# Value products in parts for four attention units, exponential sums on GpSimd, and attention loads on the sync queue, in a hybrid encoder block

## The chip, the cores and the metric

The kernel runs on one core of a Trainium2 chip. The metric is the device time of one execution in microseconds (us); lower is better. One core has TensorE (matrix products), VectorE, ScalarE, GpSimd and a sync engine that only issues transfers. The profile calls them PE, DVE, ACT, POOL and SP; PEld is TensorE's weight load.

## The reference

One layer of an encoder over 2048 tokens and 16 learned meta tokens, 1024 wide, all in float32:

```
proj = rms_norm(h) @ w_in                      # q (4 heads), k, v (2 heads each), u (4 x 128)
q, k = axial_rope(rms_norm(q)), axial_rope(rms_norm(k))
attn = softmax(q k^T / sqrt(128)) v            # every token attends to all 2064 keys
four = real(fft2(u)) @ w_fourier               # per group of 128 channels
h = h + concat(rms_norm(attn), rms_norm(four)) @ w_out
h = h + relu(rms_norm(h) @ w_up)^2 @ w_down
out = rms_norm(h), without the meta tokens
```

The change touches the attention: scores, softmax and the product with the values.

## The kernel before, in words

*Precision.* Most products split both operands into a high part in a short float32 form (type R32) and a low part, the remainder. `Split` makes them: ScalarE copies src to hi, VectorE subtracts hi from src and writes lo. `mm3` (L81 to L83) then issues three matmuls: hi with hi, hi with lo, lo with hi. A few products use whole float32 operands in one matmul instruction of the program, which the profile shows as two records. The value product of the attention (L902) is one of these.

*Attention.* Keys stand on the partitions. A unit is 256 queries of two heads (512 columns) that share a key head; there are 16 units. Each unit has 17 steps: 16 tiles of 128 keys and one of 96 rows that holds the meta keys. `scores` computes a step's scores s from keys kt and queries q in three parts; ScalarE copies them to S, two tiles to a buffer of 128x1024 (11 such buffers), and VectorE keeps the running maximum M. After a unit's last step, TensorE transposes M, VectorE reduces it, and the maximum comes back as mb. `softmax` runs 20 steps behind the scores. On an even step VectorE subtracts mb from a pair's S (L893) and ScalarE takes the exponential in place (L894). On an odd step VectorE adds the pair to the running sum acc (L898 for the first, L900 for the others: seven adds for a unit), and TensorE multiplies the two tiles with the values vn into o (L902). At step 16, acc is folded into sum, which `finish` reduces over the keys to 1/l; it passes through memory (l_d) and comes back as rb, spread over all partitions; O times rb goes to memory as parts.

*What runs beside it.* The attention is a generator of steps. Other generators fill TensorE between its steps, and `mix` spreads so many attention steps evenly over a generator's own. First comes u_pass (projection of u), then fourier (the transform, with constant tables tab in a ring of six), out_f (the Fourier half of the output product: 16 rows of 128 tokens, two halves each), then out_a for three blocks of queries (the attention half). ULEAD, FLEAD and OLEAD are the attention steps that are to be issued by the end of the first three; each block of out_a then takes STEPS_A more. In out_f, each row needs parts yh and yl of the transform's output, its squares ysq, which GpSimd adds together (L1018), a small product pys on TensorE that sums them, and rs_f, a power on GpSimd (L194). VectorE's L1046 scales out_f's product pof by rs_f and adds it to x.

*Order.* Each engine takes its instructions in the order in which the program has them; the planner that records the program sets that order from the generators and may move an instruction past others of its engine. `tc.issue_after(x)` keeps an instruction behind x. Waits between engines go by semaphores. GpSimd issues the loads of keys (kt, L754), values (vn, L763; vm, L760), queries (q, L791) and tables (tab, L608) in its own queue; nearly all other transfers of this stretch are issued by the sync engine.

Of the kernel before, what the change touches and what calls it, by code (L numbers as in the profile page):

```python
# [19 lines left out]
P = 128  # L20
# [14 lines left out]
REM = 96  # L35
# [8 lines left out]
FLEAD = 102  # L44
OLEAD = 166
AHEAD_U = 8
STEPS_A = 38
T_BUFS = 6
F_BUFS = (6, 7)
WU_BUFS = 3  # L50
P_BUFS = 5
S_BUFS = 11
A_BUFS = 5
ORDER = "1265734"
# [31 lines left out]
def ins_of(x):  # L86
    return getattr(x, "ins", x)
# [49 lines left out]
def encoder_block(ctx: ExitStack, tc: tile.TileContext, x, meta, w_in, w_f,  # L137
# [49 lines left out]
    c_fo = lambda k: cols[:, 20 + k:21 + k]  # L187

    def rstd_of(pool, ss, n, width, tag, rows=P):

        ms = pool.tile([P, n], F32, name="ms_" + tag, tag="ms_" + tag, bufs=2 if pool is tp else 4)
        nc.vector.tensor_scalar(ms[:rows], ss, 1.0 / width, EPS, op0=ALU.mult, op1=ALU.add)
        rs = pool.tile([P, n], F32, name="rs_" + tag, tag="rs_" + tag, bufs=2 if pool is tp else 4)
        nc.gpsimd.tensor_tensor(rs[:rows], ms[:rows], mhalf[:rows, :n], op=ALU.pow)  # L194
        return rs
# [400 lines left out]
    def load_tables(tr):  # L596

        src, full, rest, n_tab = sources(tr)
        rem = ft.tile([P, NG, REM], F32, name=f"rem{tr}", tag="rem", bufs=1)
        nc.vector.memset(rem, 0.0)  # L600
        for o in (0, 32, 64):
            for lo, hi in rest:
                nc.vector.tensor_copy(rem[:, :, o:o + hi - lo], src[:, :, lo:hi])
                o += hi - lo
        tabs = []
        for nt in range(n_tab):
            t = ft.tile([P, 4, CHP], R32, name=f"tab{tr}_{nt}", tag="tab", bufs=T_BUFS)[:, :, :CH]
# [99 lines left out]
    def fourier():  # L707
        for par in range(2):
# [3 lines left out]
            for g in range(NG):  # L712
# [38 lines left out]
    def load_k(u, g, c):  # L751
        n = KC + (MR if c == 3 else 0)
        kt = ap.tile([P, 2, KCP if c == 3 else KC], R32, name=f"kt_{u}_{c}", tag=f"KT{c // 3}", bufs=1 if c == 3 else 3)
        nc.gpsimd.dma_start(kt[:, :, :n], k_d[:, g, :, c * KC:c * KC + n])  # L754
        return kt

    def load_v(u, g, c):
        if c == 4:
            vt = ap.tile([P, P], R32, name=f"vm_{u}", tag="VM", bufs=1)
            nc.gpsimd.dma_start(vt[:MR], v_m[:, g])  # L760
        else:
            vt = ap.tile([P, 4, P], F32, name=f"vn_{u}_{c}", tag="VT", bufs=4)
            nc.gpsimd.dma_start(vt, v_n[:, g, 4 * c:4 * c + 4])  # L763
        return vt
# [14 lines left out]

    held = {}  # L780

    def attention():
# [5 lines left out]
        def load_q(u):  # L788
            b, g = units[u]
            q = ap.tile([P, 2, 2, 256], R32, name=f"q_{u}", tag="q", bufs=2)  # L790
            nc.gpsimd.dma_start(q, q_d[b][:, :, 2 * g:2 * g + 2])  # L791
            return q.rearrange("p l h n -> p l (h n)")
# [73 lines left out]
        def softmax(u, i):  # L866
# [4 lines left out]
            if i == NT:  # L871
# [6 lines left out]
                nc.vector.tensor_tensor(hi[32:64], S[32:64], f32v(hi[32:64]), op=ALU.subtract)  # L878
                sm = s["sum"] = ap2.tile([P, 512], F32, name=f"sum_{u}", tag="pl", bufs=1)
                nc.vector.tensor_tensor(sm, acc[:, 0], acc[:, 1], op=ALU.add)  # L880
# [10 lines left out]
            if i % 2 == 0:  # L891
                mb = s["mb"].rearrange("p (o n) -> p o n", o=1).broadcast_to([P, 2, 512])
                nc.vector.tensor_tensor(S, S, mb, op=ALU.subtract)  # L893
                held["exp"] = ins_of(nc.scalar.activation(p, S, AF.Exp, scale=ISQ))  # L894
                return
            v = vt[j // 2]
            if j == 1:
                nc.vector.tensor_tensor(acc, s["S"][0], p, op=ALU.add)  # L898
            elif j > 0:
                held["sub"] = ins_of(nc.vector.tensor_tensor(acc, acc, p, op=ALU.add))  # L900
            for e in range(2):
                nc.tensor.matmul(s["O"], v[:, 2 * j % 4 + e], p[:, e], start=i + e == 1, stop=False)  # L902

        def finish(u):
# [93 lines left out]
    def out_f():  # L998
# [6 lines left out]
        def rows(t):  # L1005
# [11 lines left out]
            for n in (2, 1):  # L1017
                nc.gpsimd.tensor_tensor(sq[:, :n], sq[:, :n], sq[:, n:2 * n], op=ALU.add)  # L1018
            ops[t] = [hi, lo, sq]
# [822 lines left out]
```

## Time and profile before

| | us |
|---|---|
| median of 3 runs | 2239.28 (2238.01 to 2241.07) |
| profiled execution, its own time | 2236.94 |
| profiled execution, span from first to last instruction | 2235.2 |

The shares of the span that each engine is busy:

| engine | busy us | share | instructions |
|---|---|---|---|
| TensorE | 2219.0 | 99% | 9890 |
| weight load | 1752.8 | 78% | 9890 |
| VectorE | 1681.4 | 75% | 2260 |
| ScalarE | 1170.8 | 52% | 1991 |
| GpSimd | 255.8 | 11% | 301 |

An engine's row in the profile names a line of the kernel, an operation, and what it writes and reads (out<-in, without buffer numbers), with its shape; after the bar stand busy us, mean ns of one, and the idle time of the engine just before, with what ended it. Rows of the timeline begin with the start and the length in us. "x4" says that four instructions are merged in the row. TensorE's matmuls are pipelined: a record of 0.39 us does not keep the next one from starting after 0.23.

### The profile page before, as it was taken

The numbers are of one execution on the slowest core, as the hardware profiler recorded it, in microseconds if no ns is written. First come the engines' busy times: TensorE is split into PE (matmuls) and PEld (weight loads), VectorE is DVE, ScalarE is ACT, GpSimd is POOL, SyncE is SP. The second block draws the span as 40 slices with busy tenths as digits, with TensorE's granted clock in tenths as the row PEclk, the third lists the DMA queues.
The fourth block names the chain that finished last, engine by engine and source line by source line (L and its number), as shares of the span: only waits on it lengthen the run. The fifth ranks groups of instructions, "written<-read, shape, count | busy, mean of one in ns | idle before, by whom it ended". The sixth has DMA issues, their size and how long they took to land.

```text
span 2235.2 us, 27654 instructions
## 1 busy us (share of the span) xinstructions
PE 2219.0 (99%) x9890; PEld 1752.8 (78%) x9890; DVE 1681.4 (75%) x2260; ACT 1170.8 (52%) x1991; POOL 255.8 (11%) x301
## 2 busy tenths in 40 slices
PE   9999999999999999999999999999999999999998
PEld 7888867777777666677888888888888888888887
DVE  6566299999888989887676778679656555796795
ACT  6554255655554667677555654334455555443243
POOL 2223101012132212110000020000100000200000
PEclk9999999999999999999999999999999999999999
DMA  7685743345346434476767585434594434955442
GB/s 244 207 264 175 255 134 90 88 114 166 118 146 206 160 95 139 133 266 231 264 225 243 198 296 192 164 125 151 213 360 151 163 138 164 344 169 160 134 130 85
DMA packets 219914, 408.08 MB, mean 183 GB/s; under 512 B 19568, under 2 KB 97776, under 8 KB 218112
## 3 DMA queue, kind: packets, MB, share of 16 engines
q1 hardware_dynamic: 192000, 343.64, 45.9%
q0 software_dynamic: 27632, 62.41, 9.1%
q8 instruction: 78, 1.28, 0.2%
q14 instruction: 60, 0.49, 0.1%
q10 hardware_dynamic: 144, 0.26, 0.0%
HBM read 260.16 MB, written 146.08 MB: 182 GB/s over the span
## 4 chain that ended last, share of the span: by engine, by line
PE 45%; DVE 3%; DMA 3%; ACT 1%; issue 1%; SPq 0%; POOLq 0%; POOL 0%; DVEq 0%; ACTq 0%
PE dx L81 5%; PE dx L83 5%; PE dx L82 5%; PE dy L81 4%; PE dy L83 4%; PE dy L82 4%; PE ux L83 3%; PE ux L82 3%; PE ux L81 3%; PE uy L81 3%; PE uy L83 3%; PE uy L82 3%; DMA f_d<-lf 2%; DMA lf<-m_d 1%; DVE wul L72 1%
## 5 line engine op out<-in xcount | busy, mean ns | idle before, releaser
L71 ACT CAST ah<-a 128x1024 fp32r<-128x1024 f32 x108 | 113.0, 1050 | 263.7 <-PE dx L82 107.2
L902 PE MATMUL o<-S,vn 128*128 128x512 f32 x512 | 242.8, 595 | 0.0
L833 ACT COPY S<-s 128x512 f32<-128x512 f32 x256 | 147.8, 587 | 143.4 <-PE s L83 136.8
L83 PE MATMUL dx<-bh,al 128*128 128x512 f32 x496 | 192.5, 388 | 0.0
L82 PE MATMUL dx<-bl,ah 128*128 128x512 f32 x496 | 192.5, 388 | 0.0
L81 PE MATMUL dx<-bh,ah 128*128 128x512 f32 x496 | 192.5, 388 | 0.0
L83 PE MATMUL ux<-bf,wul 128*128 128x512 f32 x448 | 174.3, 389 | 0.7 <-DVE wul L72 0.7
L81 PE MATMUL ux<-bf,wuh 128*128 128x512 f32 x448 | 174.6, 390 | 0.0
L82 PE MATMUL ux<-bf,wuh 128*128 128x512 f32 x448 | 174.3, 389 | 0.0
L893 DVE TENSOR_TENSOR S<-S,mb 128x1024 f32<-128x1024 f32 x128 | 153.0, 1222 | 17.6 <-ACT mb L864 17.6
L894 ACT ACTIVATE S<-S 128x1024 f32<-128x1024 f32 x128 | 134.5, 1065 | 50.0 <-DVE S L893 48.8
L72 DVE TENSOR_TENSOR al<-a,ah 128x1024 fp32r<-128x1024 f32 x108 | 131.3, 1221 | 31.7 <-ACT ah L71 31.3
L81 PE MATMUL s<-q,kt 128*128 128x512 f32 (+1 forms) x272 | 151.0, 555 | 1.8 <-DMA kt<-k_d 1.0
L81 PE MATMUL dy<-bh,ah 128*128 128x512 f32 (+1 forms) x388 | 150.5, 388 | 0.0
L82 PE MATMUL dy<-bl,ah 128*128 128x512 f32 (+1 forms) x388 | 150.5, 388 | 0.0
L83 PE MATMUL dy<-bh,al 128*128 128x512 f32 (+1 forms) x388 | 150.5, 388 | 0.0
L902 PEld LDWEIGHTS o<-S,vn 128*128 128x128 f32 x512 | 93.3, 189 | 69.1 <-issue 58.5
L81 PE MATMUL uy<-bf,wuh 128*128 128x512 f32 x320 | 124.9, 390 | 1.2 <-ACT wuh L71 1.2
L82 PE MATMUL uy<-bf,wuh 128*128 128x512 f32 x320 | 124.8, 390 | 0.0
L83 PE MATMUL uy<-bf,wul 128*128 128x512 f32 x320 | 124.7, 390 | 0.0
L1306 ACT ACTIVATE c<-c 128x512 f32<-128x512 f32 x96 | 60.5, 631 | 121.4 <-DVE c L1354 117.8
L839 DVE TENSOR_TENSOR M<-M,S 128x1024 f32<-128x1024 f32 x96 | 117.8, 1227 | 7.3 <-ACT S L833 6.1
(330 smaller groups left out, 5576.5 us busy)
## 6 DMA issues: line engine op xcount, KB each, us to landing
a<-s_d SPq DMA_DIRECT2D x84, 512.0 KB, 3.8
R<-in_w_up_dram SPq DMA_DIRECT2D x32, 1024.0 KB, 5.5
s_d<-s SPq DMA_DIRECT2D x128, 256.0 KB, 2.1
s_d<-c SPq DMA_DIRECT2D x96, 256.0 KB, 2.7
d<-in_w_down_dram SPq DMA_DIRECT2D x48, 512.0 KB, 5.1
f_d<-lf SPq DMA_DIRECT2D x56, 256.0 KB, 3.1
bf<-f_d SPq DMA_DIRECT2D x7, 2048.0 KB, 13.8
hk<-ht_d SPq DMA_DIRECT2D x24, 512.0 KB, 4.8
```

What stands on the lines that cost most here:

```text
L71: self.high = nc.scalar.copy(hi, src)
L72: self.low = nc.vector.tensor_tensor(lo, src, f32v(hi), op=ALU.subtract)
L81: nc.tensor.matmul(out, a[0], b[0], start=first, stop=False, skip_group_check=chain)
L82: nc.tensor.matmul(out, a[0], b[1], start=False, stop=False, skip_group_check=chain)
L83: nc.tensor.matmul(out, a[1], b[0], start=False, stop=last, skip_group_check=chain)
L833: nc.scalar.copy(S[:, i % 2], ps)
L839: nc.vector.tensor_tensor(M, M, S, op=ALU.max)
L893: nc.vector.tensor_tensor(S, S, mb, op=ALU.subtract)
L894: held["exp"] = ins_of(nc.scalar.activation(p, S, AF.Exp, scale=ISQ))
L902: nc.tensor.matmul(s["O"], v[:, 2 * j % 4 + e], p[:, e], start=i + e == 1, stop=False)
L1306: nc.scalar.activation(dst, src, AF.Relu)
```

## The change

Three things are done, with numbers of the order set anew.

- In units 6 to 9 (PARTS) the value product takes parts. The values' four tiles of 128x512 are split once into vp (`value_parts`); of each pair, the two 128x512 halves of the exponentials are split into hi and lo (ph and pl, five buffers together), and mm3 takes the place of the whole matmul.
- The adds of pairs 1 to 6 into acc go to GpSimd. The last, of pair 7, stays on VectorE. `on_pool` keeps GpSimd's instructions from the attention's start on in the order of the program.
- kt, vn and q are loaded by the sync queue; vm and the tables stay on GpSimd. The tables of the third transform are asked for earlier.

sum is now written into acc, and rb uses the buffer of ph. OLEAD goes from 166 to 176 and STEPS_A from 38 to 35. The operation that O's product with rb is kept behind is now the subtraction in place of the sum.

```diff
-OLEAD = 166
+OLEAD = 176
-STEPS_A = 38
+STEPS_A = 35
+PARTS = (6, 7, 8, 9)
+VP_BUFS = 5
...
+    def on_pool(call, *args, **kw):
+
+        with tc.issue_after(held["pool"]) if "pool" in held else nullcontext():
+            held["pool"] = ins_of(call(*args, **kw))
...
-        nc.gpsimd.tensor_tensor(rs[:rows], ms[:rows], mhalf[:rows, :n], op=ALU.pow)
+        if pool is tp:
+            nc.gpsimd.tensor_tensor(rs[:rows], ms[:rows], mhalf[:rows, :n], op=ALU.pow)
+        else:
+            on_pool(nc.gpsimd.tensor_tensor, rs[:rows], ms[:rows], mhalf[:rows, :n], op=ALU.pow)
...
-            nc.gpsimd.dma_start(t, c_even[tr, nt] if tr < 2 else c_odd[tr - 2, nt])
+            on_pool(nc.gpsimd.dma_start, t, c_even[tr, nt] if tr < 2 else c_odd[tr - 2, nt])
...
             sn = transform(2 * par + 1)
+            if not par:
+                load_tables(2)
...
-        nc.gpsimd.dma_start(kt[:, :, :n], k_d[:, g, :, c * KC:c * KC + n])
+        nc.sync.dma_start(f32v(kt[:, :, :n]), k_d[:, g, :, c * KC:c * KC + n])
...
-            nc.gpsimd.dma_start(vt, v_n[:, g, 4 * c:4 * c + 4])
+            nc.sync.dma_start(vt, v_n[:, g, 4 * c:4 * c + 4])
...
-            nc.gpsimd.dma_start(q, q_d[b][:, :, 2 * g:2 * g + 2])
+            nc.sync.dma_start(f32v(q), q_d[b][:, :, 2 * g:2 * g + 2])
...
+        def value_parts():
+
+            for c in range(4):
+                t = op2.tile([P, 2, 512], R32, name=f"vp_{c}", tag=f"vp{c}")
+                split(t[:, 0], t[:, 1], KV["v", PARTS[0]][c].rearrange("p a d -> p (a d)"))
+                VP.append(t.rearrange("p l (a d) -> p l a d", d=P))
...
-                sm = s["sum"] = ap2.tile([P, 512], F32, name=f"sum_{u}", tag="pl", bufs=1)
+                sm = s["sum"] = acc[:, 0]
...
-            if j == 1:
-                nc.vector.tensor_tensor(acc, s["S"][0], p, op=ALU.add)
+            if j == NT // 2 - 1:
+                nc.vector.tensor_tensor(acc, acc, p, op=ALU.add)
             elif j > 0:
-                held["sub"] = ins_of(nc.vector.tensor_tensor(acc, acc, p, op=ALU.add))
+                on_pool(nc.gpsimd.tensor_tensor, acc, s["S"][0] if j == 1 else acc, p, op=ALU.add)
+            if u in PARTS:
+                if not VP:
+                    value_parts()
+                v = VP[j // 2]
+                for e in range(2):
+                    k = 2 * j % 4 + e
+                    hi, lo = (op2.tile([P, 512], R32, name=f"p{x}{e}_" + nm, tag="vh", bufs=VP_BUFS) for x in "hl")
+                    split(hi, lo, p[:, e])
+                    mm3(nc, s["O"], (v[:, 0, k], v[:, 1, k]), (hi, lo), i + e == 1, False)
+                return
...
-                rb = ap2.tile([P, 512], F32, name=f"rb_{u}", tag="rb", bufs=1)
+                rb = ap2.tile([P, 512], F32, name=f"rb_{u}", tag="ph", bufs=1)
```

How the change moves instructions is shown at three places in the middle of out_f. First TensorE, from one row's pys to the next score. Before (L1023 is pys, L902 the whole value product of a pair's two tiles):

```order
L83 MATMUL pof_1_5967<-wfp_1_5287,yl_5857 128x512
L1023 MATMUL pys_5980<-ones,ysq_5946 128x1 [waits DVE_49,Pool_49]
L902 MATMUL o_5718<-S_10_5472,vn_2_5176 128x512 x2
L81 MATMUL s_14_5998<-q_5427,kt_3_4783 128x512 [waits Activation_49]
L82 MATMUL s_14_5998<-q_5427,kt_3_4783 128x512
```

After (lines are shifted; L83 to L85 is mm3, ph and pl are the parts of the exponentials):

```order
L85 MATMUL pof_1_6836<-wfp_1_5307,yl_6666 128x512
L1053 MATMUL pys_6849<-ones,ysq_6796 128x1 [waits PE_49,Pool_49]
L83 MATMUL o_6770<-ph_9_3_6857,vp_5309 128x512 [waits Activation_49]
L84 MATMUL o_6770<-pl_9_3_6858,vp_5309 128x512 [waits DVE_49]
L85 MATMUL o_6770<-ph_9_3_6857,vp_5309 128x512
L83 MATMUL o_6770<-ph_9_3_6864,vp_5309 128x512 [waits Activation_49]
L84 MATMUL o_6770<-pl_9_3_6865,vp_5309 128x512 [waits DVE_49]
L85 MATMUL o_6770<-ph_9_3_6864,vp_5309 128x512
L83 MATMUL s_6_6873<-q_6416,kt_1_6399 128x512 [waits Activation_49]
```

Six matmuls stand where two whole ones stood, and they wait for ScalarE and VectorE at the place; pys waits for GpSimd in both. Second, GpSimd over two rows of out_f. Before (rs_f, the two adds of the squares, and a key load):

```order
L194 TENSOR_TENSOR rs_f<-ms_f,mhalf 128x1
L1018 TENSOR_TENSOR ysq_6223<-ysq_6223 128x256
L1018 TENSOR_TENSOR ysq_6223<-ysq_6223 128x128
L754 DMA kt_0_6167<-k_d 128x2x512
L194 TENSOR_TENSOR rs_f<-ms_f,mhalf 128x1
```

After (L196 is `on_pool`, through which all of these go):

```order
L196 TENSOR_TENSOR rs_f<-ms_f,mhalf 128x1
L196 TENSOR_TENSOR acc_6281<-acc_6281,S_4_5824 128x1024
L196 TENSOR_TENSOR ysq_6440<-ysq_6440 128x256
L196 TENSOR_TENSOR ysq_6440<-ysq_6440 128x128
L196 TENSOR_TENSOR acc_6281<-acc_6281,S_6_5879 128x1024
L196 TENSOR_TENSOR rs_f<-ms_f,mhalf 128x1
L196 TENSOR_TENSOR acc_6281<-acc_6281,S_8_5932 128x1024
```

The key load is gone, and a sum stands ahead of the squares' adds and ahead of rs_f. Third, VectorE at the same place. Before (L893 is the subtraction, L839 the maximum, L900 the sum):

```order
L900 TENSOR_TENSOR acc_6156<-acc_6156,S_4_5756 128x1024
L893 TENSOR_TENSOR S_8_5840<-S_8_5840,mb_6086 128x1024
L839 TENSOR_TENSOR M_6165<-M_6165,S_4_6197 128x1024
L900 TENSOR_TENSOR acc_6156<-acc_6156,S_6_5799 128x1024
L1046 SCALAR_TENSOR_TENSOR xo_6169<-pof_0_6208,rs_f,xo_6169 128x512
L900 TENSOR_TENSOR acc_6156<-acc_6156,S_8_5840 128x1024
```

After (L913 is the subtraction, L859 the maximum, L74 the subtraction that makes pl, L1076 what was L1046):

```order
L74 TENSOR_TENSOR pl_8_3_6350<-S_2_5759,ph_8_3_6349 128x512
L913 TENSOR_TENSOR S_8_5932<-S_8_5932,mb_6204 128x1024
L1076 SCALAR_TENSOR_TENSOR xo_6247<-pof_0_6315,rs_f,xo_6247 128x512
L859 TENSOR_TENSOR M_6290<-M_6290,S_4_6312 128x1024
L74 TENSOR_TENSOR pl_8_3_6357<-S_2_5759,ph_8_3_6356 128x512
L913 TENSOR_TENSOR S_10_5987<-S_10_5987,mb_6204 128x1024
L74 TENSOR_TENSOR pl_8_5_6403<-S_4_5824,ph_8_5_6402 128x512
```

The sums are gone from VectorE's row, and two subtractions of half their width stand for each pair.

More of the change, by code (lines that the diff above doesn't have):

```diff
@@ L187, in encoder_block @@
     c_fo = lambda k: cols[:, 20 + k:21 + k]
+    held = {}
+    def on_pool(call, *args, **kw):
+        with tc.issue_after(held["pool"]) if "pool" in held else nullcontext():
+            held["pool"] = ins_of(call(*args, **kw))
     def rstd_of(pool, ss, n, width, tag, rows=P):
@@ L607, in load_tables @@
             t = ft.tile([P, 4, CHP], R32, name=f"tab{tr}_{nt}", tag="tab", bufs=T_BUFS)[:, :, :CH]
-            nc.gpsimd.dma_start(t, c_even[tr, nt] if tr < 2 else c_odd[tr - 2, nt])
+            on_pool(nc.gpsimd.dma_start, t, c_even[tr, nt] if tr < 2 else c_odd[tr - 2, nt])
             tabs.append((t[:, 0:2], t[:, 2:4]))
         t = ft.tile([P, 2, CHP], R32, name=f"tabr{tr}", tag="tabr", bufs=2)[:, :, :CH]
-        nc.gpsimd.dma_start(t[:REM], c_rem[tr])
+        on_pool(nc.gpsimd.dma_start, t[:REM], c_rem[tr])
         tabs.append(t)
@@ L759, in load_v @@
             vt = ap.tile([P, P], R32, name=f"vm_{u}", tag="VM", bufs=1)
-            nc.gpsimd.dma_start(vt[:MR], v_m[:, g])
+            on_pool(nc.gpsimd.dma_start, vt[:MR], v_m[:, g])
         else:
             vt = ap.tile([P, 4, P], F32, name=f"vn_{u}_{c}", tag="VT", bufs=4)
-            nc.gpsimd.dma_start(vt, v_n[:, g, 4 * c:4 * c + 4])
+            nc.sync.dma_start(vt, v_n[:, g, 4 * c:4 * c + 4])
         return vt
@@ L778, in a_operand @@
         return AT[b]
-    held = {}
     def attention():
@@ L798, in attention @@
         KV = {}
+        VP = []
+        def value_parts():
[3 more added lines that the diff above has]
+                VP.append(t.rearrange("p l (a d) -> p l a d", d=P))
         def loads(kind, u, c):
@@ L892, in softmax @@
                 mb = s["mb"].rearrange("p (o n) -> p o n", o=1).broadcast_to([P, 2, 512])
-                nc.vector.tensor_tensor(S, S, mb, op=ALU.subtract)
+                held["sub"] = ins_of(nc.vector.tensor_tensor(S, S, mb, op=ALU.subtract))
                 held["exp"] = ins_of(nc.scalar.activation(p, S, AF.Exp, scale=ISQ))
@@ L1017, in rows @@
             for n in (2, 1):
-                nc.gpsimd.tensor_tensor(sq[:, :n], sq[:, :n], sq[:, n:2 * n], op=ALU.add)
+                on_pool(nc.gpsimd.tensor_tensor, sq[:, :n], sq[:, :n], sq[:, n:2 * n], op=ALU.add)
             ops[t] = [hi, lo, sq]
@@ L1083, in encoder_block @@
     op_ = Lines(tc.alloc_tile_pool(name="op", bufs=1, reuse_waits="tile"), small)
+    op2 = Lines(tc.alloc_tile_pool(name="op2", bufs=1, reuse_waits="tile"), small)
     mix(out_f(), 36, FLEAD, OLEAD)
+    op2.release()
     op_.release()
```

## Prediction

> **What bounds the kernel now.** I read the page's busy times first, then the same times by stage, then TensorE's timeline, then VectorE's and GpSimd's. The page says that TensorE is busy almost all the time, which alone proves little, since the ends of its matmuls are modelled.
>
> ```profile
> PE 2219.0 (99%) x9890; PEld 1752.8 (78%) x9890; DVE 1681.4 (75%) x2260; ACT 1170.8 (52%) x1991; POOL 255.8 (11%) x301
> ```
>
> The change lies in the stretch with attention. I cut it at the first out_f product (550 us) and at the first out_a product (735 us) and call the parts A, B and C; the columns are length, then busy us of each engine.
>
> ```profile
> 253.00:550.00 297.00, 293.99 (x1375) 215.75 (x1374) 257.96 (x363) 168.30 (x281) 37.20 (x52) 1.00 0.44 124
> 550.00:735.00 185.00, 185.00 (x750) 134.23 (x748) 156.77 (x206) 95.58 (x173) 52.70 (x54) 1.00 0.49 155
> 735.00:966.00 231.00, 230.08 (x892) 154.24 (x890) 209.84 (x258) 152.84 (x247) 45.71 (x29) 1.00 0.41 130
> ```
>
> VectorE works 258 of 297 us in A, 157 of 185 in B and 210 of 231 in C, so it stands close behind TensorE everywhere. ScalarE has room. GpSimd looks empty. The granted clock is 1.00 in all three. That TensorE really is the bound shows in the distance of its starts:
>
> ```profile
> 301.43 1.88 PE L902 MATMUL o<-S,vn 128*128 128x512 f32 x4
> 303.38 0.39 PE L82 MATMUL s<-q,kt 128*128 128x512 f32 x1
> 303.61 0.40 PE L83 MATMUL s<-q,kt 128*128 128x512 f32 x1
> 304.53 1.02 PE L902 MATMUL o<-S,vn 128*128 128x512 f32 x2
> ```
>
> A matmul of a three-product form follows the next after 0.23 us (303.38 to 303.61). The four records at 301.43 are one pair of whole value products, two passes each. The first score matmul behind them has its place 0.23 ahead of 303.38, at 303.15, so the pair takes 1.72 us; with six score matmuls the step of two key tiles takes 3.10 us (301.43 to 304.53), and no time is lost between.
>
> **The parts.** *Value products in parts, units 6 to 9.* A pair becomes six matmuls, 6 x 0.227 = 1.36 us in place of 1.72. With 8 pairs in each of 4 units that is 32 x 0.36 = 11.5 us less on TensorE. The copies and subtractions that make the parts are new: 64 of the probabilities and 4 of the values, each 128x512.
>
> ```profile
> L833 ACT COPY S<-s 128x512 f32<-128x512 f32 x55 | 32.1, 584 | 43.9 <-PE s L83 42.9
> 667.37 0.68 DVE L920 TENSOR_TENSOR O<-O,rb 128x512 f32<-128x512 f32 x1
> 667.97 1.21 DVE L893 TENSOR_TENSOR S<-S,mb 128x1024 f32<-128x1024 f32 x1
> ```
>
> ScalarE: 68 x 0.584 = 39.7 us on top of its 95.6 in B, which fits. VectorE: an operation of this size passes the next after 0.60 us, so 68 x 0.60 = 40.8 us, nearly all in B.
>
> *Sums on GpSimd.* Of seven adds for each unit, six leave VectorE and one stays.
>
> ```profile
> 661.03 1.22 DVE L900 TENSOR_TENSOR acc<-acc,S 128x1024 f32<-128x1024 f32 x1
> 662.17 1.22 DVE L893 TENSOR_TENSOR S<-S,mb 128x1024 f32<-128x1024 f32 x1
> 663.30 1.22 DVE L839 TENSOR_TENSOR M<-M,S 128x1024 f32<-128x1024 f32 x1
> 664.44 1.22 DVE L900 TENSOR_TENSOR acc<-acc,S 128x1024 f32<-128x1024 f32 x1
> 665.58 0.74 DVE L1046 SCALAR_TENSOR_TENSOR xo<-pof,rs_f,xo 128x512 f32<-128x512 f32 x1
> 666.24 1.21 DVE L900 TENSOR_TENSOR acc<-acc,S 128x1024 f32<-128x1024 f32 x1
> ```
>
> On VectorE each add is worth 1.14 us (661.03 to 662.17). GpSimd shows no add of this size. Its nearest rows, of two sizes:
>
> ```profile
> L1018 POOL TENSOR_TENSOR ysq<-ysq x32: 459/794/5774, 535.4 to 697.6; 128x256 f32<-128x256 f32 x16, 128x128 f32<-128x128 f32 x16
> L414 POOL TENSOR_TENSOR cg<-cs,gqk x34: 719/762/1033, 35.0 to 222.3; 128x256 f32<-128x256 f32 x32, 96x256 f32<-96x256 f32 x2
> ```
>
> The shortest are 459 ns for 128 columns and 719 for 256, so 2.03 ns for a column and 0.2 us fixed; 1024 columns then take 0.2 + 2.08 = 2.28 us. In the Trainium skill, "GPSIMD Engine Reference" (Performance versus the Vector engine) has 4497 ns for 2048 columns; half of that, 2.25 us, is an estimate, and the sum would be the same.
>
> Alone that would be hidden. But the longest ysq record is 5774 ns, and these rows say why:
>
> ```profile
> 637.70 1.26 POOL L1018 TENSOR_TENSOR ysq<-ysq 128x256 f32<-128x256 f32 x2
> 660.47 11.31 POOL L1018 TENSOR_TENSOR ysq<-ysq 128x256 f32<-128x256 f32 x2
> 535.44 1.68 POOL L1018 TENSOR_TENSOR ysq<-ysq 128x256 f32<-128x256 f32 x2 [6.98 <-ACT ysq L1016]
> 535.68 1.11 DVE L880 TENSOR_TENSOR sum<-acc 128x512 f32<-128x512 f32 x1
> 536.71 1.48 DVE L839 TENSOR_TENSOR M<-M,S 128x1024 f32<-128x1024 f32 x1
> ```
>
> The same two adds that take 1.26 us at 637.70 take 11.31 at 660.47, beside the VectorE rows above. Those run on without a gap until L1046, which reads one operand from PSUM, and the first of the two adds ends within a microsecond of L1046's start at 665.58. The other way round, at 535.44, VectorE's L880 lasts 1.11 us where 0.68 is usual for 128x512, and L839 1.48 where 1.22 is. So a GpSimd add and a VectorE operation with two SBUF operands go one after the other, not side by side. The Trainium skill, "SBUF — State Buffer" (SBUF: two separate sides), calls it an exclusive lock that goes to whichever operation starts first, for the whole instruction. The trace agrees on the exclusion, but not on a turn for the one that waits: at 660.47 the add is passed over by operations issued after it. By strict turns the sums would be late by one VectorE operation; as the trace has it, they are late by whole runs of them.
>
> So a moved add saves VectorE 1.14 us and takes about 2.1 us of the time that both share (2.28 less the fixed 0.2). The price is bounded below by 1.14 us (no worse than before) and above by 2.28. I take 2.1, since the two-size rows are nearest in kind.
>
> *The steps.* OLEAD 176 and STEPS_A 35 bring ten attention steps (five pairs) from C into B: five times 3.10 us = 15.5 us of TensorE.
>
> *B added up.* TensorE: 185 + 15.5 - 11.5 = 189 us. VectorE: 156.8, less 24 sums x 1.14 = 27.4, plus 40.8 for parts, plus five pairs of subtraction and maximum at 2 x 1.14 = 11.4, plus some 3 for the ends of half a unit: 185 us. L1046 and the other readers of PSUM are about 26 of that:
>
> ```profile
> L893 DVE TENSOR_TENSOR S<-S,mb 128x1024 f32<-128x1024 f32 x29 | 34.9, 1234 | 4.5 <-ACT mb L864 4.5
> L900 DVE TENSOR_TENSOR acc<-acc,S 128x1024 f32<-128x1024 f32 x24 | 29.4, 1225 | 0.0
> L1046 DVE SCALAR_TENSOR_TENSOR xo<-pof,rs_f,xo 128x512 f32<-128x512 f32 x32 | 23.8, 743 | 12.8 <-PE pof L83 9.0 <-issue 3.3 <-POOL rs_f L194 0.5
> L898 DVE TENSOR_TENSOR acc<-S,S 128x1024 f32<-128x1024 f32 x4 | 4.9, 1215 | 0.0
> ```
>
> That leaves 159, less some 9 that waits on the squares' adds have already stretched: 150 us with two SBUF operands. GpSimd: 25 sums x 2.1 = 52, and 32 squares' adds at 0.4 on average = 13. Shared time: 150 + 52 + 13 = 215 us, 26 more than TensorE needs. B goes from 185 to 215: +30.
>
> *C.* Its PSUM readers are mainly one group:
>
> ```profile
> L1149 DVE SCALAR_TENSOR_TENSOR h<-poa,rs_a,h 128x512 f32<-128x512 f32 x22 | 16.4, 746 | 3.6 <-PE poa L83 1.9 <-POOL rs_a L194 0.9 <-PE pm_l L847 0.6
> ```
>
> TensorE loses the five pairs: 231 - 15.5 = 215.5. VectorE: 209.8, less five pairs at 3 x 1.14 = 17 and 3 of ends, less 34 sums x 1.14 = 39, less 16 of L1149, is 135; with 34 x 2.1 = 71 it is 206. It fits, with little to spare: -15.5.
>
> *A.* Even with all of VectorE counted, 258 - 36 x 1.14 + 36 x 2.1 = 293 us, under 297: 0.
>
> *Loads.* The key, value and query loads leave GpSimd for the sync queue.
>
> ```profile
> L754 POOL DMA_DIRECT2D kt<-k_d x20 | 14.6, 729 | 140.2 <-PE s L83 112.1 <-DMA k_d<-kt 19.2 <-PE pu L83 8.8
> L791 POOL DMA_DIRECT2D q<-q_d x16 | 11.8, 738 | 63.4 <-PE s L83 63.4
> L763 POOL DMA_DIRECT2D vn<-v_n x20 | 11.3, 571 | 126.5 <-PE o L902 126.5
> ```
>
> GpSimd is rid of 38 us and of waits of 330 us that would now hold up sums. On the sync queue the same waits stand ahead of the fetch and store of x and h, of 1/l and of O. A load is issued just behind the score that frees its buffer, so what follows it is late by at most that wait, and each has ten steps or a whole row (185 / 16, some 11 us) before its use: 0, bounded by -1 and, if four key loads each stop a row for 2 us, +8. The tables loaded earlier, the reused tiles (sum in acc, rb in ph) and the GpSimd order cost nothing by themselves: 0, from -2 (TensorE's small waits) to +3 (rb now waits for the end product of its own unit).
>
> **Sum.** 0 + 30 - 15.5 = +14.5 on the profiled execution of 2236.9 us, 2251.4. That execution lies 2.3 under the median 2239.3, so I predict 2254 us.
>
> **Rivals.** *TensorE stays the bound.* Eleven pair buffers of S let VectorE work ahead, and if the add holds the port briefly, B ends with TensorE: all of the 11.5 us stays, 2239.3 - 11.5 = 2228, to 2224 with small waits gone. It decides where a sum holds at most (189 - 150 - 13) / 25 = 1.04 us, or where room in A takes up the rest. Against it speak 2.03 ns for a column and the record of 5774 ns; for it, that GpSimd has the least work of all engines. *Sums of about 1.4 us, or part of the overrun absorbed by the lead:* 2235 to 2244, no change. *GpSimd's queue on the path.* The squares' adds and rs_f stand behind sums in the same queue, and TensorE's pys product and L1046 wait for them, once in each of 16 rows. Before, that cost L1046 0.5 us in all. If half of the rows wait for one further sum, 8 x 2.1 = 17, and PSUM readers that don't meet GpSimd's turns add up to their 26 us: 2271 to 2290. *Late key loads:* +8 on the forecast, inside its range.
>
> **Chances.** Forecast 0.36 (its own range 2244 to 2271), GpSimd's queue 0.17, TensorE bound 0.33, no change 0.14. A measurement can tell about 0.2%, 4.5 us, from nothing: faster 0.33, same 0.14, slower 0.53. The range from 2223 to 2286 takes in both ends of the price of an add.
>
> **What would show it.** After, B should be about 215 us long with TensorE's starts apart; acc records on GpSimd of 2.3 us and many far longer; VectorE subtractions and maxima over 1.3 us on average in B; waits of pys or L1046 for GpSimd. The value pairs of units 6 to 9 should start 0.36 us closer than before. A and C should keep TensorE's pace. I am wrong if sums and VectorE's operations overlap freely, if VectorE gets far enough ahead in A, or if C is also over its limit.

## The result, and the profile after

The changed kernel takes 2411.71 us (median of 4 runs, 2409.35 to 2414.83) against 2238.65 us for the kernel before on the same chip: 1.0773 times as long, interval 1.0754 to 1.0791. The prediction said 2254 us, between 2223 and 2286. The direction is right, the size is off by a factor of more than ten.

The busy times of the page, after:

```profile
PE 2265.6 (94%) x9954; PEld 1792.0 (74%) x9954; DVE 1776.0 (74%) x2232; ACT 1201.3 (50%) x2059; POOL 488.1 (20%) x341
```

The span is 2409.4 us, 174.2 longer. TensorE is busy for 46.6 us more and idle for 143.8 us where it was 16.2. So some 128 us of the loss is waiting; the other 47 are longer busy time, of matmuls that run slower. The stages A, B and C, cut as before at the first out_f and the first out_a product, and then the rest (columns: length, busy us of TensorE, weight load, VectorE, ScalarE and GpSimd, granted clock, DMA share, GB/s):

```profile
257.00:612.00 355.00, 307.21 (x1357) 221.14 (x1358) 279.12 (x326) 166.00 (x281) 130.46 (x56) 0.93 0.35 99
612.00:867.00 255.00, 213.47 (x882) 167.79 (x880) 226.83 (x263) 138.10 (x254) 113.27 (x71) 0.92 0.38 123
867.00:1137.00 270.00, 230.19 (x829) 149.89 (x827) 212.24 (x207) 142.14 (x232) 125.76 (x50) 0.93 0.32 104
1137.00:2409.00 1272.00, 1260.89 (x5601) 1043.42 (x5601) 917.54 (x1125) 629.15 (x892) 56.53 (x91) 1.00 0.58 200
```

A went from 297 to 355 us (+58), B from 185 to 255 (+70), C from 231 to 270 (+39); the start and the rest make up the other 7. The granted clock, 1.00 in all stages before, is 0.92 to 0.93 in the three. The operations that carry it, from the same kernel (sums on GpSimd, then VectorE's subtractions, maxima and parts):

```profile
L196 POOL TENSOR_TENSOR acc<-acc,S 128x1024 f32<-128x1024 f32 x80 | 242.3, 3028 | 9.8 <-ACT S L914 5.9
L913 DVE TENSOR_TENSOR S<-S,mb 128x1024 f32<-128x1024 f32 x128 | 202.3, 1611 | 18.0 <-ACT mb L884 18.0
L859 DVE TENSOR_TENSOR M<-M,S 128x1024 f32<-128x1024 f32 x96 | 142.7, 1487 | 39.2 <-ACT S L853 38.0
L74 DVE TENSOR_TENSOR pl<-S,ph 128x512 fp32r<-128x512 f32 x64 | 60.0, 942 | 0.2 <-PE o L85 0.2
L83 PE MATMUL s<-q,kt 128*128 128x512 f32 (+1 forms) x272 | 144.5, 531 | 59.4 <-ACT S L853 58.6
```

A subtraction takes 1611 ns on average where it took some 1.22 us, a part 942 where a 128x512 operation took 0.68. VectorE lost 96 sums (some 109 us), gained 68 splits (some 41 us), and is still busy longer than before (1776.0 against 1681.4 us). The view of the waits names TensorE's and VectorE's (total us, times, longest):

```profile
PE s L83 <- ACT S L853: 58.6, 19, 7.6
DVE acc L918 <- POOL acc L196: 39.9, 9, 11.8
PE o L84 <- DVE pl L74: 27.7, 16, 4.6
PE pm_m L867 <- DVE M L848: 25.8, 9, 9.2
```

L853 is ScalarE's copy of scores to S, L918 the last add of a unit, L848 the last maximum of a unit. The first of them is the largest. One such place in A, from the timelines of GpSimd, VectorE, ScalarE and TensorE:

```profile
337.12 16.43 POOL L196 TENSOR_TENSOR acc<-acc,S 128x1024 f32<-128x1024 f32 x5
338.14 3.31 DVE L856 TENSOR_TENSOR M<-S,S 128x1024 f32<-128x1024 f32 x1
341.37 9.94 DVE L913 TENSOR_TENSOR S<-S,mb 128x1024 f32<-128x1024 f32 x3
344.76 1.06 ACT L914 ACTIVATE S<-S 128x1024 f32<-128x1024 f32 x1 [5.54 <-DVE S L913]
348.11 1.06 ACT L914 ACTIVATE S<-S 128x1024 f32<-128x1024 f32 x1 [2.29 <-DVE S L913]
349.07 1.05 ACT L853 COPY S<-s 128x512 f32<-128x512 f32 x2
349.69 0.80 PE L83 MATMUL s<-q,kt 128*128 128x512 f32 x1 [7.09 <-ACT S L853]
350.29 0.63 PE L84 MATMUL s<-q,kt 128*128 128x512 f32 x1
350.71 0.63 PE L85 MATMUL s<-q,kt 128*128 128x512 f32 x1
355.40 0.41 PE L84 MATMUL pu<-hk,wh 128*128 128x512 f32 x1
355.65 0.40 PE L85 MATMUL pu<-hk,wl 128*128 128x512 f32 x1
```

Five sums stand one behind the other in 16.43 us, 3.29 each. VectorE has three subtractions in 9.94 us, 3.3 each instead of 1.14. The two engines take turns, one operation each, so VectorE runs at about a third of its rate. ScalarE's exponentials (L914) wait 5.54 and 2.29 us for these subtractions, and the copy of scores that would free PSUM stands behind them in ScalarE's queue until 349.07. So TensorE stands still for 7.09 us. It is ScalarE, idle half of its time, that hands the delay on. Afterwards TensorE's matmuls start 0.42 us apart (350.29 to 350.71) until 355.40, from where they are back at 0.25 and less. The granted clock (after ScalarE's and GpSimd's busy times) shows the same, over the wait and behind it:

```profile
343.00:349.70 6.70, 0.01 (x1) 0.01 (x1) 6.70 (x3) 2.65 (x4) 6.54 (x3) 0.66 0.26 76
349.70:355.30 5.60, 5.60 (x13) 4.45 (x14) 5.60 (x4) 2.05 (x4) 3.77 (x2) 0.50 0.01 3
```

"TensorE: Matmul & The Clock Gate" in the Trainium skill (Part 1: The HAM clock gate) says that the clock halves after an idle window of about 3.4 us and comes back after a busy one; the trace agrees, with 5.1 us at half pace here. No term of the prediction stood for this. Over the whole profile the mean clock is 0.971, before 0.999. The clock lost adds up to some 70 us, 3 before. Laid over TensorE's records, 48 of these fall into times in which a matmul runs; the others fall into waits, as in the first of the two rows, and slow no matmul.

### The profile page after: what moved, and what is told of

Read it like the earlier page. It is cut to its first block, busy times and chain, and to the rows that moved or that the text cites. A ratio compares the mean times of both kernels' runs of the same rounds, so it can differ in the third digit from the quotient of the medians.

```text
span 2409.4 us, 28063 instructions
## 1 busy us (share of the span) xinstructions
PE 2265.6 (94%) x9954; PEld 1792.0 (74%) x9954; DVE 1776.0 (74%) x2232; ACT 1201.3 (50%) x2059; POOL 488.1 (20%) x341
## 4 chain that ended last, share of the span: by engine, by line
PE 50%; DVE 0%; ACT 0%; issue 0%; POOLq 0%; POOL 0%; ACTq 0%
PE ux L85 5%; PE ux L83 5%; PE ux L84 5%; PE dx L83 5%; PE dx L84 5%; PE dx L85 5%; PE dy L84 4%; PE dy L83 4%; PE dy L85 4%; PE uy L85 4%; PE uy L83 4%; PE uy L84 4%; PE pmt L1205 0%; DVE wul L74 0%; DVE hs L1586 0%
## 5 line engine op out<-in xcount | busy, mean ns | idle before, releaser
L196 POOL TENSOR_TENSOR acc<-acc,S 128x1024 f32<-128x1024 f32 x80 | 242.3, 3028 | 9.8 <-ACT S L914 5.9
L853 ACT COPY S<-s 128x512 f32<-128x512 f32 x256 | 146.6, 584 | 145.2 <-PE s L85 115.6
L913 DVE TENSOR_TENSOR S<-S,mb 128x1024 f32<-128x1024 f32 x128 | 202.3, 1611 | 18.0 <-ACT mb L884 18.0
L83 PE MATMUL s<-q,kt 128*128 128x512 f32 (+1 forms) x272 | 144.5, 531 | 59.4 <-ACT S L853 58.6
L83 PE MATMUL dx<-bh,ah 128*128 128x512 f32 x496 | 192.7, 388 | 0.0
L85 PE MATMUL dx<-bh,al 128*128 128x512 f32 x496 | 192.6, 388 | 0.0
L932 PE MATMUL o<-S,vn 128*128 128x512 f32 x384 | 192.0, 624 | 0.0
L914 ACT ACTIVATE S<-S 128x1024 f32<-128x1024 f32 x128 | 134.0, 1061 | 84.0 <-DVE S L913 81.3
L85 PE MATMUL ux<-bf,wul 128*128 128x512 f32 x448 | 174.3, 389 | 0.7 <-DVE wul L74 0.7
L83 PE MATMUL ux<-bf,wuh 128*128 128x512 f32 x448 | 174.5, 390 | 0.0
L859 DVE TENSOR_TENSOR M<-M,S 128x1024 f32<-128x1024 f32 x96 | 142.7, 1487 | 39.2 <-ACT S L853 38.0
L74 DVE TENSOR_TENSOR al<-a,ah 128x1024 fp32r<-128x1024 f32 x108 | 131.0, 1219 | 30.3 <-ACT ah L73 30.2
L83 PE MATMUL dy<-bh,ah 128*128 128x512 f32 (+1 forms) x388 | 150.5, 388 | 0.0
L85 PE MATMUL dy<-bh,al 128*128 128x512 f32 (+1 forms) x388 | 150.5, 388 | 0.0
L1460 POOL DMA_DIRECT2D d<-in_w_down_dram x16 | 11.6, 730 | 589.3 <-PE uy L85 285.8
L83 PEld LDWEIGHTS s<-q,kt 128*128 128x128 f32 (+1 forms) x272 | 54.2, 199 | 100.8 <-ACT S L853 78.0
L83 PE MATMUL uy<-bf,wuh 128*128 128x512 f32 x320 | 124.9, 390 | 1.2 <-ACT wuh L73 1.2
```

The lines of the kernel that those rows point to most:

```text
L74: self.low = nc.vector.tensor_tensor(lo, src, f32v(hi), op=ALU.subtract)
L83: nc.tensor.matmul(out, a[0], b[0], start=first, stop=False, skip_group_check=chain)
L85: nc.tensor.matmul(out, a[1], b[0], start=False, stop=last, skip_group_check=chain)
L196: held["pool"] = ins_of(call(*args, **kw))
L853: nc.scalar.copy(S[:, i % 2], ps)
L859: nc.vector.tensor_tensor(M, M, S, op=ALU.max)
```

## Experiments: which part does it

**The sums back on VectorE (e1), with parts and sync loads kept.**

```diff
-            if j == NT // 2 - 1:
-                nc.vector.tensor_tensor(acc, acc, p, op=ALU.add)
-            elif j > 0:
-                on_pool(nc.gpsimd.tensor_tensor, acc, s["S"][0] if j == 1 else acc, p, op=ALU.add)
+            if j > 0:
+                nc.vector.tensor_tensor(acc, s["S"][0] if j == 1 else acc, p, op=ALU.add)
```

> The changed kernel with all seven adds of a unit back on VectorE; parts, sync-queue loads and the new step numbers stay. Theory port (GpSimd's sums and VectorE's two-operand work exclude each other, in A, B and C alike): nearly all of the 173 us go; B is then set by VectorE, 157 + 41 + 14 = 212 us, so about 2250 us. Rival loads (sync-queue loads come late and TensorE's scores wait): stays above 2350. Rival parts (the subtractions that make pl stand right ahead of their matmuls): 2300 or more, with the loss in B alone.

Measured: 2255.28 us, ratio 1.0075 (1.0060 to 1.0090). So 156 us of the loss belong to the sums.

**No parts (e2): `PARTS = ()`, sums on GpSimd and sync loads kept.**

> The changed kernel with whole value products in all units; sums on GpSimd and sync-queue loads stay. Theory port: A and C stay as long as after the change (355 and 270 us), B loses VectorE's 41 us of splits and the 28 us in which value products waited for pl, so about 2350 us. Rival loads: the same A and C, so this run alone doesn't tell them apart. Rival parts: below 2270 us.

Measured: 2371.2 us, 1.0593 (1.0578 to 1.0609); A 359, B 214 and C 270 us. The sums lose 132 us without any parts (against e4, below), and A and C are as long as in the whole change.

**Loads back on GpSimd (e3): the three `nc.sync.dma_start` of kt, vn and q as they were.**

> The changed kernel with the key, value and query loads on GpSimd's queue again; sums on GpSimd and parts stay. Theory port: 2400 us or more, since the sums now also stand behind loads that wait for score products. Rival loads: falls to 2260 or less.

Measured: 2418.78 us, 1.0811 (1.0793 to 1.0829), 7 us above the whole change.

**Loads alone (e4): e1's diff and `PARTS = ()` together.**

> Sums on VectorE, whole value products: of the change only the sync-queue loads, the order of GpSimd's queue, the earlier tables and the step numbers are left. Theory port: 2239 us within 10. Rival loads: 2330 or more.

Measured: 2239.15 us, 1.0006 (0.9996 to 1.0016). The loads and the new order cost nothing by themselves. From e4 to e1 the parts cost 16 us; from e2 to the whole change they cost 40. I read this as VectorE having no room left there; no run shows that by itself.

## Experiments: what about the sums does it

**No sums at all (e5).** e2's kernel, with the six adds on GpSimd left out; VectorE's seventh adds a constant to the last pair.

```diff
-                nc.vector.tensor_tensor(acc, acc, p, op=ALU.add)
-            elif j > 0:
-                on_pool(nc.gpsimd.tensor_tensor, acc, s["S"][0] if j == 1 else acc, p, op=ALU.add)
+                nc.vector.tensor_tensor(acc, p, ones.rearrange("p (o n) -> p o n", o=1).broadcast_to([P, 2, 512]), op=ALU.add)
```

> No parts, sync-queue loads; the six adds of a unit are done on no engine (the sums are left out; the seventh add takes a constant for the running sum). A baseline for the next two. Both theories: TensorE is the bound, 2230 to 2239 us; VectorE's relief by 6 x 1.14 us for each unit is worth next to nothing.

Measured: 2238.87 us, 1.0002 (0.9993 to 1.0012). VectorE's work falls by some 100 us and the time does not move: without parts there is nothing to gain from taking the sums off VectorE, wherever they go. Losses below are counted from this run, or from e4 where the sums stay in.

**Unrelated products in their place (e6).** To e5, GpSimd adds one column of the pair (`tick`, which sets the moment) and squares a tile of its own that nobody waits for (the lines that set up the two tiles are left out).

```diff
+            elif j > 0:
+                on_pool(nc.gpsimd.tensor_tensor, tick, p[:, 0, :1], p[:, 1, :1], op=ALU.add)
+                on_pool(nc.gpsimd.tensor_tensor, dump, dump, dump, op=ALU.mult)
```

> As the run with the six adds left out, but for each of them GpSimd does one operation of the same size on a buffer of its own, behind a one-column operation that waits for the exponentials. No engine waits for its result. Theory exclusion (the time that both need is what costs): 2330 to 2371 us, nearly as with the real sums. Rival lateness (it costs because S buffers, the seventh add and the unit's end wait for late sums): 2260 or less.

Measured: 2309.49 us, 1.0319 (1.0304 to 1.0335). No engine waits for the product, and 71 us are lost. The attention is not quite out of it: tick reads the pair, and the squares' adds and rs_f stand in the same queue. The next run keeps both of these.

**Stores without reads (e7): two memsets of 128x1024 in place of the product.**

> As the run before, but GpSimd's operation only writes: two memsets of 128x1024 in place of one product. Theory exclusion as the Trainium skill has it (a VectorE operation with two SBUF operands meets only a GpSimd operation that reads SBUF): 2230 to 2245. If any GpSimd work of this length costs: 2300 or more.

Measured: 2235.07 us, 0.9989 (0.9979 to 0.9998). The groups of GpSimd's operations and VectorE's subtractions, first with e6's products, then with these memsets:

```profile
L196 POOL TENSOR_TENSOR dump<-dump 128x1024 f32<-128x1024 f32 x96 | 224.1, 2334 | 0.0
L916 DVE TENSOR_TENSOR S<-S,mb 128x1024 f32<-128x1024 f32 x128 | 175.3, 1407 | 19.2 <-ACT mb L887 19.1
```

```profile
L196 POOL MEMSET dump<- 128x1024 f32 x192 | 182.8, 952 | 5.5
L916 DVE TENSOR_TENSOR S<-S,mb 128x1024 f32<-128x1024 f32 x128 | 151.3, 1220 | 17.4 <-ACT mb L887 17.3
```

With the memsets GpSimd is busy for 183 us and VectorE keeps its 1220 ns; with the products, 224 us, it has 1407. It is GpSimd's reading of SBUF that excludes VectorE's operations with two SBUF operands, not its being busy, nor its writing. The Trainium skill says so in "SBUF — State Buffer" (Who interferes with whom), and this run shows it. L1076, which reads one operand from PSUM, takes 741 ns in the changed kernel; the same operation took 743 before.

**Half of the sums (e8: `if j > 3` in place of the last pair alone, so that GpSimd makes three of a unit's seven), and the three in a tile of their own that VectorE adds in at the end (e9), so that no sum is waited for in mid-unit.**

> No parts; the first three adds of a unit on GpSimd, the other four on VectorE. Exclusion with a cost for each add: half of the 132 us of six adds, about 2305 us. Exclusion with a threshold (it costs only where the shared time runs out): 2245 to 2280.

> No parts; GpSimd adds pairs 0 to 3 into a tile of its own, VectorE pairs 4 to 7 into acc, and one more VectorE add joins them at the unit's end: as many adds on each engine as with three sums on GpSimd (2312 us), but no add in mid-unit waits for GpSimd. If lateness is half of the price of a sum: about 2275. If the price is exclusion alone: 2300 to 2315.

Measured: 2311.59 us, 1.0330 (1.0314 to 1.0345), and 2312.08 us, 1.0333 (1.0319 to 1.0347). Half of the sums cost 72 us, 55% of six. VectorE's wait for GpSimd's sums is 43.4 us in e8 and 15.2 in e9, and the time is the same; the wait in mid-unit is not the price. Nor does it matter only how full a stage is: by the prediction's terms, VectorE's and GpSimd's work with half of the sums is 275 us in A, of 297, and 190 in C, of 215. Yet against e4, A grows from 295 to 332 us in e8 and C (up to the last value product) from 218 to 252. B stays at 200; no run shows why it is spared.

**Shorter turns.** e10 is e6 with the product in two of 128x512. e11 is e6 with two one-operand copies of 128x1024 in place of the product.

> As the run with unrelated adds (2309 us), with two operations of 128x512 in place of each of 128x1024. If the price is the total time that GpSimd holds: 2300 to 2315. If it is the length of a single wait of VectorE (one turn at a time, 2.1 us): 2260 to 2285.

> As the run with unrelated adds, with two copies of 128x1024 in place of each product: GpSimd reads one operand and not two. If every GpSimd operation that reads SBUF excludes VectorE's two-operand work, as the Trainium skill states: 2290 to 2320. If only operations with two operands do: 2232 to 2242.

Measured: 2281.92 us, 1.0189 (1.0173 to 1.0204), and 2278.37 us, 1.0179 (1.0165 to 1.0193). Halving costs 43 us in place of 71, though the halves together are no less work (1029 ns for each at the shortest, 1885 for the whole product). A copy excludes too.

**Parts in two units (e12): `PARTS = (7, 8)` and e1's diff.**

> Sums on VectorE, sync-queue loads, parts in units 7 and 8 alone. TensorE needs 2 x 8 x 0.36 = 5.8 us less; VectorE's work in B grows by 20 us to 189 of about 195. If that room is enough: 2232 to 2235, a little faster than before. If VectorE at 95% already holds TensorE up, as with four units: 2238 to 2246.

Measured: 2235.18 us, 0.9988 (0.9979 to 0.9997). Beside e7, which leaves the sums out, this is the only run whose interval lies below 1, and the fastest kernel that computes everything. Two units fit beside out_f, four do not. The gain, 0.1%, is below what I called tellable.

## Experiments: why a real sum costs twice e6's product

**Real sums that nobody uses (e13).** To e5, GpSimd adds each pair into its own tile.

```diff
+            elif j > 0:
+                on_pool(nc.gpsimd.tensor_tensor, dump, dump, p, op=ALU.add)
```

> No parts; GpSimd adds each of the six pairs into a tile of its own, over all units, so it reads S as the real sums do and holds each S buffer until it is done, but no engine waits for the result and no tile of the sums has to come free. If holding S is what makes a real sum cost twice an unrelated product: about 2371 us, as with the real sums. If the chain through acc does (the first sum of a unit waits until the last unit's acc has been read, the seventh add waits for GpSimd): about 2309.

Measured: 2348.26 us, 1.0493 (1.0474 to 1.0511). 109 of e2's 132 us are there although VectorE waits for no sum.

**Two accumulator tiles (e14: `bufs=2` for acc) and twelve pair buffers (e15: `S_BUFS = 12`), both on e2.**

> No parts, real sums on GpSimd (2371 us), with two acc tiles in turn, so that a unit's first sum doesn't wait for the last unit's acc. If that wait carries the difference to the unrelated products: 2310 to 2335. If holding S does: 2360 to 2375.

> No parts, real sums on GpSimd (2371 us), with twelve S buffers for eleven. If S buffers that come free late carry the difference: 10 to 40 us less. If acc does: 2365 to 2375.

Measured: 2374.27 us, 1.0606 (1.0590 to 1.0623), and 2379.01 us, 1.0626 (1.0607 to 1.0645); e2 had 2371.2. Neither a second tile nor one more buffer helped, though each took away the wait that it was meant for. The first sums of units wait 20.5 us in e2 until the old acc has been read, and not at all in e14. ScalarE's copies wait 27.8 us in e2 for a buffer that a sum still holds, and 5.6 in e15. So both of the causes that I had offered fell here.

**e2's sums cut up: four adds of 128x256 (e16), eight of 128x128 (e17).**

```diff
-                on_pool(nc.gpsimd.tensor_tensor, acc, s["S"][0] if j == 1 else acc, p, op=ALU.add)
+                for h in range(4):
+                    c = (slice(None), h // 2, slice(h % 2 * 256, h % 2 * 256 + 256))
+                    on_pool(nc.gpsimd.tensor_tensor, acc[c], (s["S"][0] if j == 1 else acc)[c], p[c], op=ALU.add)
```

> The second experiment's kernel (sums on GpSimd, loads on the sync queue, no parts), with each of the six sums of a unit made by four adds of 128x256 in place of one of 128x1024. The sums are all there. Theory of the turn's length: beside a backlog on GpSimd, VectorE's operations with two SBUF operands go one for one with GpSimd's, so the loss follows how long a single GpSimd operation holds. An add of 256 columns takes 719 ns by its row in the profile of before, a quarter of some 2.9 us for a whole sum: 2300 to 2325 us. Rival, the total time held or the lateness of the sums counts: GpSimd's whole work for a sum grows from 2.3 to 2.9 us, so no less than the 2371 us of the undivided sums, and up to 2400.

> The same with eight adds of 128x128 for a sum. Theory of the turn's length: an add of 128 columns takes 459 ns, so a turn is shorter still: 2275 to 2300 us, faster than with quarters though GpSimd's own work for a sum grows to 3.7 us. Rival, total time held or lateness: 2371 us or more, and slower than with quarters.

Measured: 2382.99 us, 1.0650 (1.0634 to 1.0666), and 2432.31 us, 1.0867 (1.0849 to 1.0885). Both went against my theory. The groups of e16 say why, VectorE's subtractions, its last add of a unit, and GpSimd's quarters:

```profile
L913 DVE TENSOR_TENSOR S<-S,mb 128x1024 f32<-128x1024 f32 x128 | 170.9, 1373 | 23.8 <-ACT mb L884 23.8
L918 DVE TENSOR_TENSOR acc<-acc,S 128x1024 f32<-128x1024 f32 x16 | 21.1, 1321 | 97.3 <-POOL acc L196 97.3
L196 POOL TENSOR_TENSOR acc<-acc,S 128x256 f32<-128x256 f32 x320 | 299.6, 970 | 0.7 <-ACT S L914 0.6
```

The subtractions did become shorter, 1373 ns against 1629 in e2. But each quarter waits for its own turn, so a sum takes 4 x 970 ns = 3.9 us in place of 3.0, sums come later, and VectorE stands before its last add for 97.3 us (e2 has 45.3, e17 144.5).

**The cut without that wait (e18): e13's adds in four of 128x256.**

```diff
-                on_pool(nc.gpsimd.tensor_tensor, dump, dump, p, op=ALU.add)
+                for h in range(4):
+                    c = (slice(None), h // 2, slice(h % 2 * 256, h % 2 * 256 + 256))
+                    on_pool(nc.gpsimd.tensor_tensor, dump[c], dump[c], p[c], op=ALU.add)
```

> The kernel e13_sums_unused with each of its adds (GpSimd adds every pair's exponentials into a tile that nobody reads) cut into four of 128x256. As there, the sums of exponentials are left out and no operation of VectorE waits for GpSimd. Theory now: an uncut add holds 2.1 us in one turn, four quarters hold the same 2.1 us in four turns of about 0.5, and with a backlog each VectorE operation loses one turn; in e16 that gain was lost again where VectorE waited for the late sums (97 us for the last add, 45 in the uncut kernel). Without these waits the loss falls from e13's 109 us to between that of e10 (43) and e6 (71): 2280 to 2315 us, with VectorE's subtractions at about 1.35 us on average in place of 1.68. Rival, what counts is the total time held, or the buffers of S that a slow GpSimd frees late: 2348 us as in e13, or more.

Measured: 2297.47 us, 1.0268 (1.0251 to 1.0286): 59 us lost in place of 109. GpSimd's adds and VectorE's subtractions, first in e13, then in e18:

```profile
L196 POOL TENSOR_TENSOR dump<-dump,S 128x1024 f32<-128x1024 f32 x96 | 301.7, 3143 | 167.2 <-ACT S L917 163.3
L916 DVE TENSOR_TENSOR S<-S,mb 128x1024 f32<-128x1024 f32 x128 | 210.5, 1682 | 21.0 <-ACT mb L887 21.0
```

```profile
L196 POOL TENSOR_TENSOR dump<-dump,S 128x256 f32<-128x256 f32 x384 | 456.9, 1223 | 121.6 <-ACT S L917 121.6
L916 DVE TENSOR_TENSOR S<-S,mb 128x1024 f32<-128x1024 f32 x128 | 174.8, 1403 | 18.7 <-ACT mb L887 18.6
```

GpSimd is busy half as long again (456.9 against 301.7 us), and the kernel is 51 us faster. In the view of the waits, ScalarE's exponentials wait for subtractions 79.5 us in e13 and 38.7 in e18, and TensorE's scores for the copies behind them 51.5 and 20.6:

```profile
ACT S L917 <- DVE S L916: 79.5, 40, 6.7
PE s L83 <- ACT S L856: 51.5, 15, 7.2
```

```profile
ACT S L917 <- DVE S L916: 38.7, 37, 2.3
PE s L83 <- ACT S L856: 20.6, 15, 3.7
```

Two things set the price of a sum on GpSimd. One is the time that VectorE's operations lose at GpSimd's turns, and it goes with the length of a single operation of GpSimd (e13 against e18, e6 against e10). VectorE's busy time shows it. Over the 1579.0 us of e5 it grows as follows (us):

| | VectorE's growth | loss | difference |
|---|---|---|---|
| e6, products | 123 | 71 | 53 |
| e10, half products | 99 | 43 | 56 |
| e11, copies | 93 | 40 | 54 |
| e13, unused sums | 166 | 109 | 57 |
| e18, unused quarters | 106 | 59 | 47 |

In all five the loss is VectorE's growth less some 50 us. It looks as if VectorE could take so much more before TensorE feels it; this is read from five runs and was not tried.

The other is the lateness of a sum that VectorE itself waits for. In e2 VectorE's busy time grows by 141.5 us, and it stands for 45.3 before its last adds; the 132 us lost are again some 54 less than the two together. This wait grows when the operation is cut (e16 and e17 against e18). There the count no longer comes out: growth and wait are 176 and 191 us, the losses 144 and 193. ScalarE's copies also wait for buffers that sums still hold, 37.3 us in e16, 44.4 in e18 and 84.4 in e17; what that adds in e17 no run separates.

## Why the prediction was wrong, point by point

*Right: the size of one add.* The prediction had 2.28 us alone and 2.1 shared. The tile view of the changed kernel gives shortest, median and longest in ns:

```profile
L196 POOL TENSOR_TENSOR acc<-acc,S x80: 2343/3201/9727, 300.8 to 1132.1; 128x1024 f32<-128x1024 f32 x80
```

The shortest is 2.34. Where the engines take turns, VectorE's operation takes 3.3 in place of 1.14, so a sum holds it for some 2.15.

*Right: the exclusion.* e6 and e7 show it; they differ only in GpSimd's operation, one that reads SBUF and one that only writes it. *Only partly right: the way turns are given.* The prediction set "as the trace has it" against strict turns. After the change both occur. At 337.12 the turns are strict, for five sums on end. At 459.05 a sum is passed over by eight operations of VectorE, which run on at full rate (the rows leave three of them out), and its record lasts 9.7 us:

```profile
456.56 12.21 POOL L196 TENSOR_TENSOR acc<-acc,S 128x1024 f32<-128x1024 f32 x2
458.98 1.21 DVE L859 TENSOR_TENSOR M<-M,S 128x1024 f32<-128x1024 f32 x1
460.72 3.48 DVE L913 TENSOR_TENSOR S<-S,mb 128x1024 f32<-128x1024 f32 x3
464.13 1.21 DVE L859 TENSOR_TENSOR M<-M,S 128x1024 f32<-128x1024 f32 x1
```

What decides between the two is not settled. Strict turns make VectorE late and passing over makes the sums late; of the two, the prediction named the second alone.

*Wrong: "A, 0", since 293 us of VectorE and GpSimd go under 297.* I have worked out from the trace the time in which VectorE or GpSimd, or both, had an operation: 287 us in A, 241 in B, 238 in C. The sums of the prediction were 293 for A, and for B and C, with their PSUM readers, 241 (215 and 26) and 222 (206 and 16). So the work was added up to within 16 us. The failed step is the one behind it: that a stage in which such a sum fits runs at TensorE's pace. A used its shared time for 81% of its 355 us. Over a whole stage 293 fits into 297; over a stretch like the 16.43 us from 337.12 on, where five sums come in a row, it does not. There TensorE waits, and what it has not done then isn't made up in a stage where it had 3 us to spare. A measured +58. Nor is it a matter of the last 3 us: e8's A and C had 20 us and more to spare by such sums, and grew by 37 and 34.

*Wrong for the same reason: "C fits, with little to spare", -15.5.* It measured +39; a C over its limit was among the signs of being wrong that the prediction gave. The moved steps did take their time out of C: in e1, with sums on VectorE, C takes 214 us, and the prediction had 215.5.

*Wrong in size: "B, +30".* It measured +70. Taking the longest of the engines' sums as the length of the stage lacked the waits between them: 27.7 us in which a value product waits for pl, 9.3 us before the last add in B, and a clock of 0.92.

*Missing: the clock.* It follows the stalls and adds to them: at most the 48 us in which matmuls run at the lower clock in the changed kernel (none before), 18 of the 71 us lost in e6 (mean clock 0.989) and 28 of the 109 in e13 (0.983).

*The parts.* By the prediction's own terms, parts without moved sums give VectorE 212 us in B (156.8 + 40.8 + 11.4 + 3) and, with C's -15.5, 2251 us; e1 measured 2255, with 222 us in B. TensorE's own term held where nothing waits: in e12, matmuls of a value product start at 602.79, 603.02 and 603.26, 0.23 apart. TensorE has less to do but VectorE, with 207 of the 222 us busy, doesn't let it show; in e12, with half of the parts, B takes 198 us.

*Loads.* 0 with a bound of +8; e4 measured 1.2 us above the kernel before beside it (2237.97), within what can be told.

*The rivals.* "TensorE stays the bound" and "no change" needed a sum to hold VectorE for at most 1.04 us (the first) and about 1.4 (the second); it is 2.15. "GpSimd's queue on the path" had the mechanism in the wrong place. In B these are the waits of pys, and of the scaled add for rs_f:

```profile
L1053 PE MATMUL pys<-ones,ysq 128*128 128x1 f32 x32 | 4.7, 215 | 0.3 <-POOL ysq L196 0.3
L1076 DVE SCALAR_TENSOR_TENSOR xo<-pof,rs_f,xo 128x512 f32<-128x512 f32 x32 | 23.7, 741 | 3.7 <-PE pof L85 2.7 <-POOL rs_f L196 0.9
```

They cost 1.2 us, not 17. The queue's order hurts at the other end: GpSimd stands for 108.5 us ahead of rs_f until VectorE has made ms_f (124 us with its other waits there), and the sums are behind it. They were ready: for 82 of the 124 us, the exponentials that the next sum reads were already done. At 708.45, for one, GpSimd has stood for 9.57 us, and the exponentials for the sum behind it were done at 686.59:

```profile
685.53 1.06 ACT L914 ACTIVATE S<-S 128x1024 f32<-128x1024 f32 x1 [1.61 <-DVE S L913]
708.45 0.55 POOL L196 TENSOR_TENSOR rs_f<-ms_f,mhalf 128x1 f32<-128x1 f32 x1 [9.57 <-DVE ms_f L201]
708.97 2.65 POOL L196 TENSOR_TENSOR acc<-acc,S 128x1024 f32<-128x1024 f32 x1
```

Other engines feel little of that in B: VectorE's last adds wait for sums for 9.3 us there, ScalarE's copies for 9.1.

*Still open.* What sets the 50 us that VectorE can take; why B is spared in e8; the rule of the turns; and how much would be left if ScalarE's copies of scores stood ahead of the exponentials that wait. That path is read from the timeline and from the waits of e13 and e18; no run moved the copies.

## What to carry to other kernels

An elementwise operation moved from VectorE to an idle GpSimd is not free even where GpSimd has all the room: if it reads SBUF, VectorE can lose its whole length at a turn, here 2.15 us against the 1.14 us saved. That the two engines' work, added up over a stage, fits under TensorE's does not make it free: half of the sums left 20 us and more in two stages by that reckoning and cost 37 and 34 us there. Look at the fullest 10 us and not at the sum, and add to a stall of several us the slower matmuls behind it (here 12 of them, 0.42 us apart in place of 0.23, after 7.1 us). And leave the work out first, as e5 did: if the time does not move, there is nothing to be gained by moving it.

## What the runs showed of the hardware that was not expected

- GpSimd's 128x1024 stores without a read, at 952 ns each and 183 us in all, leave VectorE's two-operand operations at 1220 ns; 192 copies, with one operand read, cost 40 us.
- Cutting a GpSimd operation makes VectorE faster and GpSimd slower at once: four quarters take 4.9 us (4 x 1223 ns) where one add takes 3.14, both beside VectorE.
- An add that reads two tiles takes 2.34 us at the shortest (changed kernel), a product of a tile with itself 1.89 (e6), for the same 128x1024.
- After a stall of 7 us TensorE ran 12 matmuls at half pace (0.42 us apart, granted clock 0.50) before it was back.
